# Four token tiles of an encoder trunk loaded column-major and normed there

## The chip, the cores and the metric

The kernel runs on one core of a Trainium2 chip. The metric is device time in microseconds (us) for one launch; lower is better. Each version is timed in several runs, and one further execution is recorded by the hardware profiler.

## The reference

One layer of a hybrid encoder over 1024 tokens (a grid of 16 x 64) with 1024 channels:

```python
h = layer_norm(x, emb_ln_g, emb_ln_b)
q, k, v, z_a, u, z_b, g_a, g_b = split(h @ w_in)          # 512 x6, 1024 x2 columns
y_a = neighbourhood_attention(q, k, v, rpb) * silu(z_a)   # 8 heads, windows of 8 x 16 keys
y_b = (rg_lru(conv(u), forward) + rg_lru(conv(u), backward)) * silu(z_b)
m = sigmoid(g_a + b0) * (y_a @ w_ba) + sigmoid(g_b + b1) * (y_b @ w_bb)
out = layer_norm(ALPHA * h + m @ w_out, ln_g, ln_b)
```

The embedding's norm h is needed twice: with channels on the partitions, as an operand of the input projection, and with tokens on the partitions, at the very end, in `ALPHA * h`.

## The kernel before

The tokens are cut into eight tiles of 128 (16 grid rows x 8 grid columns). A product of two float32 matrices is made from float32r halves: each operand is split into a high part (a cast, mostly on ScalarE) and a low part (the rest, a subtraction on VectorE or GpSimd), and three products are added up (`mm3`: high-high, low-high, high-low).

All engines work in the order in which the program text issues the instructions (TensorE, VectorE, ScalarE, GpSimd and the SP queue that issues DMAs are all scheduled by hand), so one line that waits holds up what stands behind it on its engine.

The first stage (0 to 82 us) norms the tokens and makes v and the first q heads. For a tile i of 4 to 7:

- `load_x(i)` loads 128 tokens x 1024 channels. `ln_sums` takes mean and variance on VectorE and a root on ScalarE; `ln_scale` applies them on ScalarE (L255); `ln_g` multiplies by the gain and adds the bias in four 128x512 operations on GpSimd (L261).
- `keep(i)` stores the result to `h_d` in DRAM, from where the last stage reads it.
- `turn` makes eight 128x128 transposes on TensorE into PSUM (L272, four for each half `kk` of the channels); `turn_hi` casts the high part on ScalarE (L281), `turn_lo` makes the low part on VectorE. They fill columns of `B11`, `B12`, `B21`, `B22`: first index, half of the channels; second, tiles 0 to 3 or 4 to 7.
- `t_full(i)` makes the sums of a Strassen-like scheme (seven block products instead of eight) on VectorE: t1, t2, t3 (L302 to L305), `t_last` t4; `t_hi` casts them on ScalarE (L314), `t_lo` makes the lows on GpSimd. They fill `T1` to `T4`.

Between these stand the products: `v_part(i, kind, ks)` ("h", "w", "a": high-high, low weights, low tokens; eight products each, L328), `q_part(m, n)`; their outputs are taken out of PSUM by `v_hi`/`v_lo`, `q_hi`/`q_lo` (ScalarE, VectorE L360). The outputs in the pool `ps0` take its four banks b0 to b3 as the list `places` deals them: v_part(2) to (7) take 3, 2, 3, 2, 0, 1 with q_part(1,0) on 1, and then q_part(0,1) 2 and q_part(1,1) 3. Before the block products, `s_load`, `s_sum` (VectorE, L386), `s_hi`, `s_lo` prepare the weights of pair 0.

The second stage (82 to 425 us) runs 17 pairs of weight columns, seven block products each (a11, a12, s2, s1, s3, s4, a22); a11 and a12 use B11 and B21, s2, s1, s3, a22 use T2, T1, T3, T4. Its PSUM pools `psd` (two banks) and `ps6` (six) take the place of `ps0` and `pst`.

The third stage (about 425 to 532 us) is attention, in units: 8 heads x 8 units, a unit being about 1.6 us. A unit has TensorE score one tile of the next head (`score`), turn a tile of probabilities (`turned`), multiply by values; VectorE adds the bias (`biased`) and makes lows, ScalarE takes exponentials (`exped`) and highs (`turned_hi`). `load_head` loads k, q and bias two heads ahead. Products of the other branch fill up TensorE. The last stage makes the output projection and the last norm; `z_load` reads `h_d`.

Lines that the profile gives as L128 are `lo_of`, a subtraction on whichever engine it is given; L134 is the product of `mm3`.

Of the kernel before, what the change touches and what calls it, by code (L numbers as in the profile page):

```python
# [10 lines left out]
F32 = mybir.dt.float32  # L11
# [24 lines left out]
HEAD_AT = 116  # L36
LO_POOL = ("a11", "a22")
# [9 lines left out]
SM_CW, SM_CB, SM_GB, SM_LAM, SM_BM, SM_N = 0, 16, 20, 36, 44, 60  # L47
# [20 lines left out]
def encoder_kernel(ctx, tc, x, gb1, gb, w_qk, w_v, w_s, w_ba, w_bb, w_gate, smalls, bias, w_out, out):  # L68
# [43 lines left out]
    smh = cst.tile([P, SM_N], F32, name="smh")  # L112
# [152 lines left out]

    tps = {}
# [27 lines left out]
    def t_full(i):  # L294
# [6 lines left out]
        A.copy(t3, tp4(i, 0))  # L301
        V.tensor_tensor(t1, tp4(i, 0), f(B11[0], i), ALU.subtract)  # L302
        V.tensor_tensor(t1, t1, f(B11[1], i), ALU.subtract)
        V.tensor_tensor(t2, tp4(i, 1), t1, ALU.subtract)
        V.tensor_tensor(t3, tp4(i, 1), t3, ALU.subtract)  # L305
# [63 lines left out]
    def s_load(p, *names):  # L369
        for z, o in enumerate(names if p < N_PAIR else ()):  # L370
            if p:
                t = wsp.tile([P, 4, P], F32, tag=o, bufs=2 if o == "a22" else 1, name=f"{o}_{p}f")[:]
            else:
                if z == 0:
                    place = dict(pool=ln, tag="x", bufs=5) if o == "a21" else dict(pool=wpl, tag="ws", bufs=1)
                    both = place.pop("pool").tile([P, 2, 4, P], F32, name=f"{o}_{p}f", **place)
                t = both[:, z]
# [86 lines left out]
    qk_load(1)  # L464
    load_x(6)
# [32 lines left out]
    for c, pl in zip((4, 3, 1, 2), hts):  # L498
        Ts[c] = pair(pl, [P, 4, HALF], f"ht{c}", tag=f"ht{c}")
    T1, T2, T3, T4 = (Ts[c] for c in (1, 2, 3, 4))  # L500
# [7 lines left out]
    def tile_in(i):  # L508
        for kk in BOTH:
            turned_in(i, kk)  # L510

# [4 lines left out]
    def ln_next(i):  # L516
        ln_sums(i)
        ln_scale(i)
        ln_g(i)

# [9 lines left out]
    ln_scale(4)  # L530
    ln_g(4)
    qk_prep(1)
# [5 lines left out]
    ln_next(5)  # L538
    for kind in "hwa":
        v_part(2, kind, KS)  # L540
    keep(4)
    ln_next(6)
    v_hi(2)
    for kind in "hw":
        v_part(3, kind, KS)
    v_lo(2)
    v_store(2)
    keep(5)
    tile_in(4)
    tile_lo(4)  # L550
    ln_next(7)
    v_part(3, "a", KS)
    t_full(4)
# [3 lines left out]
    keep(6)  # L557
    q_part(0, 0, slice(256, HALF))
    tile_in(5)
    q_hi(0, 0)  # L560
    t_hi(4, 2, 1, 3)
    t_lo(4, 2, 1, 3)
    tile_lo(5)
    q_lo(0, 0)
    q_store(0, 0)
    keep(7)
    t_full(5)
    q_part(1, 0)
    q_hi(1, 0)
# [3 lines left out]
    t_lo(5, 2, 1, 3)  # L573
    for kind in "hwa":
        v_part(4, kind, KS)
    tile_in(6)
    v_hi(4)
    tile_lo(6)
    v_lo(4)
    v_store(4)  # L580
    t_full(6)
    t_hi(6, 2, 1, 3)
    t_lo(6, 2, 1, 3)
    for kind in "hwa":
        v_part(5, kind, KS)
    s_load(0, "a11", "a12")
# [1177 lines left out]
```

## Time and profile before

| | |
|---|---|
| time, median of 3 runs | 663.57 us (663.17 to 663.83) |
| profiled execution, own time | 663.47 us |
| its span, first to last instruction | 661.7 us |
| granted TensorE clock | 0.997 |
| busy: PE / DVE / ACT / POOL | 649.3 / 524.5 / 388.7 / 395.6 us |
| DMA | 113.42 MB, 171 GB/s mean |

PE is TensorE's matmuls, PEld its weight loads, DVE VectorE, ACT ScalarE, POOL GpSimd, SP the queue that issues DMAs. A row of a timeline gives start, duration, engine, line, operation, output<-input and shape, and in brackets the idle time before it and what ended it. Equal instructions in a row are merged (x8); durations of neighbours overlap a little, so the distance of starts is what an instruction costs its engine.

### The profile page before, as it was taken

What the parts mean: (1) busy time and instruction counts of PE and PEld (TensorE: products, weight loads), DVE (VectorE), ACT (ScalarE), POOL (GpSimd) and SP (SyncE); (2) the same over time, 40 slices, a digit from 0 to 9 for tenths busy, and PEclk for the clock granted to TensorE, in tenths of its full rate; (3) what the DMA queues carried; (4) which work ended last, traced back from release to release, by engine and by line L of the source; (5) the groups of instructions that cost most, each with busy time, mean ns of one, the idle gap of its engine ahead of it and who ended that gap; (6) DMA issues with size and microseconds to landing.
All of it is one profiled execution on the core that took longest, in us unless ns stands there. A gap on an engine that the chain in (4) does not pass through costs nothing.

```text
span 661.7 us, 9467 instructions
## 1 busy us (share of the span) xinstructions
PE 649.3 (98%) x3119; PEld 542.3 (82%) x3119; DVE 524.5 (79%) x860; ACT 388.7 (59%) x686; POOL 395.6 (60%) x311
## 2 busy tenths in 40 slices
PE   8999999999999999999999999999999999999994
PEld 6888888888888888888788888889888888888883
DVE  7978767986899599879987697177887876994776
ACT  5564433356786677777666834277777734573242
POOL 6799263434676476658556455012552649989857
PEclk9999999999999999999999999999999999999998
DMA  8747607133334133532361548898977288333023
GB/s 326 275 140 247 192 33 230 42 113 125 128 115 140 48 112 108 180 109 83 132 218 60 191 161 286 302 350 272 355 267 243 66 307 295 111 115 127 24 104 128
DMA packets 52481, 113.42 MB, mean 171 GB/s; under 512 B 5504, under 2 KB 9936, under 8 KB 50896
## 3 DMA queue, kind: packets, MB, share of 16 engines
q1 hardware_dynamic: 51968, 112.28, 49.0%
q8 instruction: 25, 0.41, 0.3%
q10 hardware_dynamic: 464, 0.53, 0.2%
q14 instruction: 24, 0.20, 0.1%
HBM read 77.11 MB, written 35.68 MB: 170 GB/s over the span
## 4 chain that ended last, share of the span: by engine, by line
PE 87%; DVE 7%; POOL 2%; issue 1%; ACT 1%; DMA 0%; POOLq 0%; SPq 0%; DVEq 0%; ACTq 0%
PE a L134 32%; PE mb L134 13%; PE s L134 12%; PE x L134 6%; PE w L134 5%; PE v L328 4%; PE acc L1156 3%; PE s L1108 3%; PE pt L1130 3%; PE q L134 2%; PE g L806 2%; POOL x L261 1%; DVE ws_l L128 1%; PE tp L272 1%; DVE uc L764 1%
## 5 line engine op out<-in xcount | busy, mean ns | idle before, releaser
L134 PE MATMUL a<-ht_h,ws_h 128*128 128x512 f32 x136 | 53.1, 391 | 0.0
L134 PE MATMUL a<-ht_h,ws_l 128*128 128x512 f32 x136 | 53.0, 389 | 0.0
L134 PE MATMUL a<-b_h,wa_l 128*128 128x512 f32 x136 | 53.0, 389 | 0.0
L134 PE MATMUL a<-ht_l,ws_h 128*128 128x512 f32 x136 | 52.9, 389 | 0.0
L134 PE MATMUL a<-b_h,wa_h 128*128 128x512 f32 x136 | 52.9, 389 | 0.0
L134 PE MATMUL a<-b_l,wa_h 128*128 128x512 f32 x136 | 52.9, 389 | 0.0
L1118 DVE CUSTOM_DVE_ANT_0 sc<-s,bias 128x384 f32<-128x384 f32 (+1 forms) x64 | 33.4, 523 | 20.2 <-PE s L1108 9.1
L1137 ACT CAST pt_h<-pt 128x384 fp32r<-128x384 f32 x64 | 29.0, 453 | 23.8 <-PE pt L1130 19.3
L1123 ACT ACTIVATE p<-sc,summ 128x384 f32<-128x384 f32 (+1 forms) x64 | 37.9, 592 | 5.5 <-DVE summ L1118 5.1
L134 PE MATMUL mb<-ya,wb_h 128*128 128x512 f32 x128 | 39.7, 390 | 0.0
L914 POOL CAST wb_h<-wb 128x512 fp32r<-128x512 f32 x9 | 7.0, 779 | 48.2 <-DMA wb<-in_w_bb_dram 30.4
L128 DVE TENSOR_TENSOR pt_l<-pt,pt_h 128x384 fp32r<-128x384 f32 x64 | 33.2, 519 | 1.9 <-ACT pt_h L1137 1.5
L328 PE MATMUL v<-wv,b_h 128*128 128x512 f32 x128 | 32.6, 397 | 0.4 <-ACT b_h L427 0.4
L128 POOL TENSOR_TENSOR ht_l<-t,ht_h 128x512 fp32r<-128x512 f32 x16 | 22.0, 1407 | 18.3 <-ACT ht_h L314 18.3
L1522 POOL TENSOR_TENSOR z<-z,gb 128x512 f32<-128x512 f32 (+2 forms) x23 | 27.6, 1215 | 8.6 <-ACT z L1517 7.7
L1108 PE MATMUL s<-ks,qs 128*128 128x384 f32 (+1 forms) x128 | 31.6, 328 | 0.0
L134 PEld LDWEIGHTS a<-ht_h,ws_h 128*128 128x128 f32 x136 | 25.5, 188 | 5.9 <-issue 0.4
L1130 PEld LDWEIGHTS pt<-ident,p 128*128 128x128 f32 x176 | 23.2, 140 | 8.5
L134 PEld LDWEIGHTS a<-b_h,wa_h 128*128 128x128 f32 x136 | 25.5, 188 | 5.4
L134 PEld LDWEIGHTS a<-ht_l,ws_h 128*128 128x128 f32 x136 | 25.5, 188 | 5.4
L134 PEld LDWEIGHTS a<-b_h,wa_l 128*128 128x128 f32 x136 | 25.5, 188 | 5.3
L134 PEld LDWEIGHTS a<-b_l,wa_h 128*128 128x128 f32 x136 | 25.5, 188 | 5.3
(542 smaller groups left out, 2259.4 us busy)
## 6 DMA issues: line engine op xcount, KB each, us to landing
ks<-k_d SPq DMA_DIRECT2D x8, 1024.0 KB, 8.4
h_d<-x SPq DMA_DIRECT2D x8, 512.0 KB, 2.9
v_d<-vs SPq DMA_DIRECT2D x8, 512.0 KB, 3.2
q_d<-q SPq DMA_DIRECT2D x8, 512.0 KB, 3.2
ga_d<-ga SPq DMA_DIRECT2D x16, 256.0 KB, 2.1
gb_d<-gb SPq DMA_DIRECT2D x16, 256.0 KB, 2.5
k_d<-k SPq DMA_DIRECT2D x8, 512.0 KB, 4.0
qs<-q_d SPq DMA_DIRECT2D x8, 512.0 KB, 4.6
```

What stands on the lines that cost most here:

```text
L128: eng.tensor_tensor(lo, full, hi.bitcast(F32), ALU.subtract)
L134: PE.matmul(o, a, b, start=first and i == 0, stop=last and i == len(prods) - 1, skip_group_check=not (first and last))
L328: PE.matmul(vos[i][:], a, wv[kind == "w"][k][:], start=vn[i] == 0, stop=vn[i] == 23)
L806: PE.matmul(o[:, n, :], w[:, 2 * d + b, :], us[b][:, n * HALF:(n + 1) * HALF], start=z == 0, stop=z == 1)
L914: G.tensor_copy(hi[:], st[:])
L1108: PE.matmul(o[:, :P * len(near(t))], q[:, t * P:(t + 1) * P], k[:, z, keys], start=z == 0, stop=z == 1)
L1118: V.tensor_tensor_reduce(s[:, :w], o[:, :w], heads[h][2][:, b0:b0 + w], -1.0, 3.0e38, ALU.add, ALU.min, accum_out=sums[h][0][:, t:t + 1])
L1123: A.activation(probs[h % 2][t][:], scs.pop((h, t))[:, :w], AF.Exp, bias=sums[h][0][:, t:t + 1], scale=-1.0, accum_out=sums[h][1][:, t:t + 1])
L1130: PE.transpose(tp[:, n * P:(n + 1) * P], probs[h % 2][t][:, z * P:(z + 1) * P], ident[:])
L1137: A.copy(pt[0][:, span(b)], tps[h, b][:, :P * len(near(b))])
L1156: PE.matmul(acc[n][:, lo - n * HALF:hi - n * HALF], vvs[h // 2][:, b, h % 2, :], pt[:, a:a + hi - lo], start=b in (1, 6) and z == 0, stop= ...
L1522: G.tensor_tensor(z, z, gbs[c, n][:, part], (ALU.mult, ALU.add)[c])
```

## The change

Tiles 4 to 7 are also passed in transposed (`xt`, channels on the partitions) and loaded in that form; the token-major tile is still loaded, for its mean and variance alone. These two numbers per token are spread over all partitions by two TensorE transposes of a broadcast column (`spread`), copied to SBUF, and applied to the transposed tile by GpSimd (`centred`: subtract, multiply; four 128x512 operations). Gain and bias are per partition there and applied by ScalarE in eight 128x128 activations (`affine`), with the casts of the high part behind. The low parts (`lows_t`) and `t_full` then read the tile in SBUF. The eight transposes of these tiles, their `ln_scale`, `ln_g` and `keep` go.

The token-major normed form of tiles 4 to 7, which the last stage reads from `h_d`, is made in the attention stage, for 128 channels of all four tiles at a time (eight times, m): load, scale on ScalarE by the kept statistics, gain and bias on GpSimd, store. Several loads and `t_last` stand elsewhere in the order, and `finish_a` uses one buffer instead of two.

```diff
+TOKENS_AT = ((-2, 7, 8, 11), (4, 12, 13, 17))
...
+    def load_xt(i):
+        pl, tag = {4: (hts[3], "ht2h"), 5: (hts[0], "ht4h"), 7: (hts[0], "ht4l")}.get(i, (None, None))
+        if pl:
+            both_xt[0] = pl.tile([P, 2, NK, P], F32, tag=tag, name=f"xt{i}")
+        xts[i] = both_xt[0][:, int(i == 6)]
+        SP.dma_start(xts[i], xt[i - 4])
+    def stats_t(i):
+        ln_sums(i)
+        sts_rest(i)
+    def sts_rest(i):
+        ln_rstd(i)
+        st, mv, sd, ve = sts[i]
+        V.tensor_scalar(kept[:, 2 * i - 8:2 * i - 7], mv[:, 0:1], -1.0, sd, ALU.mult, ALU.mult)
+        V.tensor_copy(kept[:, 2 * i - 7:2 * i - 6], sd)
+    def spread(i):
+        bcp[i] = pst.tile([P, HALF], F32, tag="bank", name=f"bcp{i}")
+        for z, col in enumerate((sts[i][1][:, 0:1], sts[i][2])):
+            PE.transpose(bcp[i][:, z * P:(z + 1) * P], col.to_broadcast([P, P]), ident[:])
+    def centred(i):
+        bcs[i] = wsp.tile([P, 2, P], F32, tag=f"s{i - 3}", name=f"bc{i}")
+        A.copy(bcs[i][:], bcp[i][:, :2 * P].rearrange("p (z t) -> p z t", z=2))
+        for kk in range(2):
+            t = xts[i][:, 4 * kk:4 * kk + 4, :]
+            for z, op in enumerate((ALU.subtract, ALU.mult)):
+                G.tensor_tensor(t, t, bcs[i][:, z:z + 1, :].to_broadcast([P, 4, P]), op)
+    def affine(i):
+        for k in range(NK):
+            g, b = (sm[:, SM_LN + 8 * z + k:SM_LN + 8 * z + k + 1] for z in range(2))
+            A.activation(xts[i][:, k, :], xts[i][:, k, :], AF.Identity, bias=b, scale=g)
+            if k % 4 == 3:
+                A.copy(blocks[k // 4][1][0][:, :, ti(i)], xts[i][:, k - 3:k + 1, :])
+    def lows_t(i):
+        for kk in range(2):
+            hi, lo = blocks[kk][1]
+            lo_of(V, lo[:, :, ti(i)], xts[i][:, 4 * kk:4 * kk + 4, :], hi[:, :, ti(i)])
...
-        A.copy(t3, tp4(i, 0))
-        V.tensor_tensor(t1, tp4(i, 0), f(B11[0], i), ALU.subtract)
+        u0, u1 = xts[i][:, 0:4, :], xts[i][:, 4:8, :]
+        V.tensor_tensor(t1, u0, f(B11[0], i), ALU.subtract)
         V.tensor_tensor(t1, t1, f(B11[1], i), ALU.subtract)
-        V.tensor_tensor(t2, tp4(i, 1), t1, ALU.subtract)
-        V.tensor_tensor(t3, tp4(i, 1), t3, ALU.subtract)
+        V.tensor_tensor(t2, u1, t1, ALU.subtract)
+        V.tensor_tensor(t3, u1, u0, ALU.subtract)
...
+    def tokens_in(m):
+        cols = slice(m * P, (m + 1) * P)
...
+        SP.dma_start(hw[m][:], x[4:, :, cols].rearrange("i p c -> p i c"))
+        SP.dma_start(rows[0][:, m % 2], gb1[:, :, cols].broadcast_to([P, 2, P]))
+    def tokens_scaled(m):
+        for i in range(4):
+            A.activation(hw[m][:, i], hw[m][:, i], AF.Identity, bias=kept[:, 2 * i:2 * i + 1], scale=kept[:, 2 * i + 1:2 * i + 2])
+    def tokens_gained(m):
+        for z, op in enumerate((ALU.mult, ALU.add)):
+            G.tensor_tensor(hw[m][:], hw[m][:], rows[0][:, m % 2, z:z + 1].to_broadcast([P, 4, P]), op)
+    def tokens_out(m):
+        SP.dma_start(h_d[4:, :, m * P:(m + 1) * P].rearrange("i p c -> p i c"), hw[m][:])
...
+    for m in range(NK):
+        for unit, f in zip(TOKENS_AT[m % 2], (tokens_in, tokens_scaled, tokens_gained, tokens_out)):
+            todo.setdefault(16 * (m // 2) + unit, []).append(lambda f=f, m=m: f(m))
```

The new order of the first stage, from where the two differ (products at the places of before are left out where nothing around them changes; `qk_load(1)` is followed by `load_xt(4)`):

```python
load_xt(5); keep(2); keep(3)
...                                     # tiles 2 and 3 turned; ln_sums(4); v_lo(0)
sts_rest(4); tile_lo(2); tile_lo(3); v_lo(1); v_store(1)
load_x(7); load_xt(6); load_xt(7)
v_part(2, "h"); v_part(2, "w"); spread(4); centred(4); qk_prep(1); stats_t(5)
v_part(2, "a"); stats_t(6); v_hi(2); v_part(3, "h"); spread(5); centred(5); v_lo(2); v_store(2)
v_part(3, "w"); spread(6); centred(6); stats_t(7); affine(4)
v_part(3, "a"); lows_t(4); t_full(4); v_hi(3); v_lo(3); v_store(3)
q_part(0, 0, second half); spread(7); centred(7); affine(5); q_hi(0, 0)
t_hi(4, 2, 1, 3); t_lo(4, 2, 1, 3); q_lo(0, 0); q_store(0, 0); lows_t(5); t_full(5)
q_part(1, 0); affine(6); q_hi(1, 0); q_lo(1, 0); q_store(1, 0)
t_hi(5, 2, 1, 3); t_lo(5, 2, 1, 3); lows_t(6); t_full(6); t_last(4); s_load(0, "a11", "a12")
v_part(4); affine(7); v_hi(4); t_hi(6, 2, 1, 3); t_lo(6, 2, 1, 3); s_load(0, "a21", "a22"); v_lo(4); v_store(4)
v_part(5); lows_t(7); t_full(7); v_hi(5); v_lo(5); t_last(5); s_load(1, "a21"); v_store(5)
t_hi(7, 2, 1, 3); t_lo(7, 2, 1, 3)
v_part(6); s_sum(0, ...); v_hi(6); v_lo(6); s_load(1, "a12"); v_store(6)
v_part(7); v_hi(7); v_lo(7); s_load(1, "a11"); v_store(7)
...                                     # s_hi, s_lo of pair 0, q_part(0, 1), q_part(1, 1) as before
t_hi(4, 4); t_hi(5, 4); t_last(6); t_last(7); t_hi(6, 4); q_hi(1, 1); q_lo(1, 1); q_store(1, 1); t_hi(7, 4)
t_lo(4..7, 4)
```

More of the change, by code (lines that the diff above doesn't have):

```diff
@@ L464, in encoder_kernel @@
     qk_load(1)
+    load_xt(4)
     load_x(6)
@@ L537, in encoder_kernel @@
     load_x(7)
[L538 to L542, printed above, removed]
+    load_xt(6)
+    load_xt(7)
+    v_part(2, "h", KS)
+    v_part(2, "w", KS)
+    spread(4)
+    centred(4)
+    qk_prep(1)
+    stats_t(5)
+    v_part(2, "a", KS)
+    stats_t(6)
     v_hi(2)
-    for kind in "hw":
-        v_part(3, kind, KS)
+    v_part(3, "h", KS)
+    spread(5)
+    centred(5)
     v_lo(2)
     v_store(2)
[L548 to L551, printed above, removed]
+    v_part(3, "w", KS)
+    spread(6)
+    centred(6)
+    stats_t(7)
+    affine(4)
     v_part(3, "a", KS)
+    lows_t(4)
     t_full(4)
```

105 lines of the change are left out of this document (55 added, 50 removed).

## The prediction

> **What bounds the kernel now.** I read the page's busy times first, then TensorE's waits, then the timeline of each engine over 16 to 100 us, the only stretch whose order changes apart from attention.
>
> ```profile
> PE 649.3 (98%) x3119; PEld 542.3 (82%) x3119; DVE 524.5 (79%) x860; ACT 388.7 (59%) x686; POOL 395.6 (60%) x311
> ...
> PE a L134 <- DVE w L839: 0.4, 1, 0.4
> ...
> PE tp L272 <- POOL x L261: 0.3, 1, 0.3
> ...
> 4.01 2.74 PE L213 MATMUL gps<-ident,gb_col 128*128 128x128 f32 x16
> 6.58 0.50 PE L204 MATMUL clock<-zero 128*128 128x128 bf16 x6
> ...
> 26.39 3.92 PE L328 MATMUL v<-wv,b_h 128*128 128x512 f32 x16
> 30.14 1.98 PE L328 MATMUL v<-wv,b_l 128*128 128x512 f32 x8
> ...
> 41.18 0.60 PE L272 MATMUL tp<-ident,x 128*128 128x128 f32 x4
> 42.10 0.66 PE L272 MATMUL tp<-ident,x 128*128 128x128 f32 x4 [0.32 <-POOL x L261]
> 42.51 0.48 PE L134 MATMUL q<-b_h,wqk_h 128*128 128x512 f32 x1
> ...
> 48.07 3.79 PE L328 MATMUL v<-wv,b_h 128*128 128x512 f32 x16
> ...
> 53.51 1.03 PE L272 MATMUL tp<-ident,x 128*128 128x128 f32 x8
> 54.30 3.92 PE L328 MATMUL v<-wv,b_h 128*128 128x512 f32 x16
> ...
> 82.53 0.39 PE L134 MATMUL a<-b_h,wa_h 128*128 128x512 f32 x1
> ...
> 85.25 0.39 PE L134 MATMUL a<-b_h,wa_h 128*128 128x512 f32 x1
> ```
>
> TensorE is busy for 98% and after its first 10 us it waits twice, 0.32 us at tile 5's transposes and 0.4 for a scan's input near 320. So the time falls by what TensorE no longer issues, as long as the other engines still feed it in time; every wait that appears counts in full. In the timeline, columns are start, duration, engine, line, op; starts of neighbours give the true price: eight transposes of a tile take 54.30 - 53.51 = 0.79 us.
>
> **What TensorE saves.** 32 transposes go: three tiles at 0.79, and tile 5 at 42.51 - 41.18 = 1.33 with its wait, 3.70 us. Two transposes of a broadcast column per tile come, eight in all. Their nearest row is the 16 of L213, (6.58 - 4.01)/16 = 0.16 us each; if the slow ones were only a cold start, they cost the 0.10 us of an ordinary transpose. So 0.8 to 1.3 us return, and TensorE alone gains 2.4 to 2.9; I take 2.6. Without any wait the first product a11 would start at 79.9 instead of 82.53 and a12 at 82.65 instead of 85.25.
>
> **What the others get instead.** ScalarE loses a 128x1024 scaling and a copy per tile, and gains the copy of the two broadcast rows and eight 128x128 activations. GpSimd keeps four 128x512 operations a tile (centre and scale instead of gain and bias). VectorE keeps its count but not its operands: the lows of both halves and three of t_full's four subtractions read the transposed tile from PSUM until now, and from SBUF afterwards. That is the edit which matters, for these rows:
>
> ```profile
> 50.21 2.98 POOL L261 TENSOR_TENSOR x<-x,gb 128x512 f32<-128x512 f32 x2
> ...
> 51.58 1.62 POOL L261 TENSOR_TENSOR x<-x,gb 128x512 f32<-128x512 f32 x1
> ...
> 50.09 0.68 DVE L302 TENSOR_TENSOR t<-tp,b_h 128x512 f32<-128x512 f32 x1
> 50.80 1.24 DVE L303 TENSOR_TENSOR t<-t,b_l 128x512 f32<-128x512 f32 x1
> 52.08 0.69 DVE L304 TENSOR_TENSOR t<-tp,t 128x512 f32<-128x512 f32 x1
> ...
> 81.82 0.69 DVE L310 TENSOR_TENSOR t<-t,b_l 128x512 f32<-128x512 f32 x1
> ...
> 186.05 1.75 POOL L128 TENSOR_TENSOR wa_l<-a_5f,wa_h 128x512 fp32r<-128x512 f32 x1
> 188.78 1.74 POOL L128 TENSOR_TENSOR wa_l<-a_6f,wa_h 128x512 fp32r<-128x512 f32 x1
> 186.56 1.78 DVE L386 TENSOR_TENSOR s_6f<-a_6f 128x512 f32<-128x512 f32 x1
> ```
>
> L302, L303 and L304 have one shape and run beside GpSimd. The two that read PSUM take 0.68 and 0.69 us; the one with both operands in SBUF takes 1.24, and GpSimd's operation beside it takes 1.62 instead of 1.3. The same form takes 0.69 (L310) while GpSimd rests. So the two engines take turns: VectorE waits for the running GpSimd operation, then the next one of GpSimd waits for VectorE. Where both have a queue (186 us), each takes about 1.75. VectorE's 0.60 us operation then costs 1.75.
>
> Before, four of VectorE's two-SBUF operations (L303), and the first two sums of s_sum, met GpSimd; the rest ran while it was idle:
>
> ```profile
> 34.41 2.39 POOL L128 TENSOR_TENSOR wqk_l<-wqk_s,wqk_h 128x1024 fp32r<-128x1024 f32 x1
> 36.76 16.44 POOL L261 TENSOR_TENSOR x<-x,gb 128x512 f32<-128x512 f32 x12
> 53.16 11.76 POOL L128 TENSOR_TENSOR ht_l<-t,ht_h 128x512 fp32r<-128x512 f32 x9
> 66.92 4.25 POOL L128 TENSOR_TENSOR ht_l<-t,ht_h 128x512 fp32r<-128x512 f32 x3 [2.01 <-ACT ht_h L314]
> 87.43 5.95 POOL L128 TENSOR_TENSOR ht_l<-t,ht_h 128x512 fp32r<-128x512 f32 x4 [16.26 <-ACT ht_h L314]
> ...
> 69.01 1.01 DVE L386 TENSOR_TENSOR s_0f<-a_0f 128x512 f32<-128x512 f32 x1
> 70.05 1.67 DVE L386 TENSOR_TENSOR s_0f<-s_0f,a_0f 128x512 f32<-128x512 f32 x1
> ...
> 77.96 0.69 DVE L360 SCALAR_TENSOR_TENSOR q<-q,q 128x512 fp32r<-128x512 f32 x1 [1.44 <-ACT q L355]
> ...
> 83.36 0.69 DVE L360 SCALAR_TENSOR_TENSOR q<-q,q 128x512 fp32r<-128x512 f32 x1 [0.84 <-ACT q L355]
> ...
> 59.51 1.66 ACT L314 CAST ht_h<-t 128x512 fp32r<-128x512 f32 x3 [3.10 <-DVE t L304]
> ...
> L1137 ACT CAST pt_h<-pt x64: 359/479/482, 435.5 to 530.4; 128x384 fp32r<-128x384 f32 x48, 128x256 fp32r<-128x256 f32 x16
> ```
>
> **The walk.** I go through the new order of each in-order engine by hand: GpSimd 1.29 us per 128x512, VectorE 0.60, 1.75 each when both queue, ScalarE 0.24 per 128x128 (0.36 and 0.48 at 256 and 384 columns leave 0.12 per 128) and 0.53 per 128x512 cast. Up to tile 7's statistics little changes. spread(4) stands behind the 16 products of v_part(2) from 26.39, at 30.1; with 0.4 for it and 0.4 for the copy, centred(4) starts on GpSimd at 31.0 and ends at 36.15, and qk_lo (2.39) ends at 38.5. Tile 7's statistics are no longer behind tile 4's lows; their root is off ScalarE at 39.0, and affine(4) follows there until 41.9.
>
> From here VectorE's queue sets the pace, since GpSimd always has centred(5), (6), (7) and then the twelve t_lo operations waiting. VectorE ends lows_t(4) at 43.4, t_full(4) at 50.4, v_lo(3) and q_lo(0,0) at 51.6, lows_t(5) at 53.9, t_full(5) at 60.9, q_lo(1,0) at 61.5, lows_t(6) at 64.4, t_full(6) at 70.3 (GpSimd is briefly empty there), t_last(4) at 72.6, v_lo(4) at 73.2, lows_t(7) at 76.1: 22 two-SBUF operations in 35 us, where they would take 13 alone.
>
> TensorE against it: v_part(4) at 47.1 and v_part(5) at 52.5 find their lows. v_part(6) reaches its low products near 61.6 and waits for lows_t(6), about 1.9 us in two pieces. v_part(7) reaches its low products at 69.0 and waits for lows_t(7), 5.4 us and then 0.8; it ends at 77.1, before near 71.6 (82.53 less two q_parts of 5.44, the price of 24 products by 53.51 - 48.07). q_part(0,1) takes the PSUM bank of v_part(5) (the list `places` deals 2, to both), which v_lo(5) behind t_full(7) frees at 79.1. It and q_part(1,1) take 10.9 us and end at 90.05.
>
> VectorE goes on: t_last(5) against t_lo(7) to 82.1, s_sum to 85.7, v_lo(6), v_lo(7) to 86.9, five s_lo to 89.9, q_lo(0,1) 90.8, two s_lo 91.95, then t_last(6) and t_last(7) beside T4's lows on GpSimd to 97.8, and q_lo(1,1) to 98.4. After `ps0` and `pst` are given up, `psd` takes banks 0 and 1, so a11 falls on bank 2 (q_part(0,1)) and a12 on bank 3 (q_part(1,1)). Before, these were free at 78.65 and 84.05, ahead of 82.53 and 85.25. Now a11 waits until 90.85 and a12 until 98.45. T1 to T3 end by 83.3 and T4 near 99, ahead of their products (a22 comes 16 us behind a11). Sum: 98.45 - 85.25 = 13.2 us later, the 2.6 gain already inside.
>
> **The queues.** SP: load_xt(4) goes after qk_load(1) at 20 us, xt 5, 6, 7 in place of four stores of h_d, 512 KB for 512 KB; xt(4) has eleven us until GpSimd reads it at 31, more than the 9.1 that twice as many bytes (ks, below) needed at most. What stands behind x(7) on SP are xt(6), xt(7), ahead of v_store(2) only, which no one waits for until q_hi. Nothing charged. kept adds one 128x1 operation per tile on VectorE, about 0.2, inside the walk.
>
> **Attention.** Eight times a load of 256 KB and rows of 128 KB, four 128x128 activations, two GpSimd operations, a store.
>
> ```profile
> 446.00:459.00 13.00, 13.00 (x82) 11.58 (x82) 10.36 (x30) 9.60 (x28) 1.90 (x2) 1.00 0.80 270
> 459.00:472.00 13.00, 13.00 (x82) 11.41 (x81) 10.60 (x32) 9.57 (x27) 10.67 (x10) 1.00 0.97 347
> ...
> 436.02 1.46 SPq L936 DMA_DIRECT2D ks<-k_d  x1
> ...
> DMA to landing us min/median/max: 5.0/8.4/9.1
> ...
> 447.21 0.40 PE L1108 MATMUL s<-ks,qs 128*128 128x256 f32 x2
> ```
>
> The columns are PE, PEld, DVE, ACT, POOL, clock, DMA share, GB/s. ScalarE has 3.4 us free of 13 and gets 1.2 at one time, behind exped, with the next turned_hi 0.5 to 1.1 us off; GpSimd has 8 us free in every 25; VectorE's operations there read PSUM, so GpSimd does not slow them. The DMA share is the tight one: ks of head 2 lands by 445.1 at the slowest, 2.1 us ahead of its use at 447.21, and 384 KB put in front of it take 384/340 = 1.1 us. The SP queue can wait for a store that is still in flight before it reloads the same tile (three slots, 4.7 us, later), with a reload that is first read over seven slots on. Charged at 0, bound 1.5, and below by 0 as nothing on TensorE's path is taken away here.
>
> **Sum.** 663.47 (the profiled execution; span 661.7 and 1.8 around it; 0.1 under the median of the runs) + 13.2 = 676.7 us.
>
> **Rivals.**
> Only one of the two bank waits binds: the buffers fall otherwise than I read them, or VectorE's chain is a few us shorter because GpSimd loses turns. Then a11 sets the shift, 90.85 - 82.53 = 8.3: 671.8 us, with a spread from 665 to 673. For it: no wait on a bank shows in this trace; against: the banks' order follows from the list.
>
> It is faster, 660.9 us (660.4 to 661.8): VectorE's chain stays ahead of TensorE, so only the 2.6 counts. The point from which this decides is lows_t(7) at 67 and q_lo(1,1) at 82.6, so 43 two-SBUF operations and nine that read PSUM (31 us alone) must fit into 42 us from 40.5; that is so if an operation costs under 0.85 instead of 1.75. For it: all sums of VectorE's and GpSimd's own work fit, L303's first took 1.02 only. Against: every row where both queue.
>
> The saved transposes are hidden or eaten to the last (no change): the chain's end would have to hit 85.2 by chance.
>
> Slower still: TensorE runs slowly after a long stop. The 16 transposes at 4 us took 0.16 each, those at 53 us 0.10; at that rate for the 5 us from its first work at 1 us to 6 us, a restart loses 5 x (1 - 0.10/0.16) = 1.9. Only the stop in front of a12 (4.9 us) is on the path: 678.6 us. The Trainium skill's "TensorE: Matmul & The Clock Gate", Part 1, says that the array halves its clock after an idle window of about 3.4 us and needs as long to return; by that, an estimate of 1.7 us would be lost. No stop of such length after the start is in this trace, so it stays a rival.
>
> **Chances.** The walk, with and without the slow restart, 673 to 681: 0.45 (0.12 of it the restart). One bank wait or a shorter chain, 665 to 673: 0.28. Faster: 0.20. Within 0.2%, which is about what a measurement can tell from no change: 0.05. Above 681: 0.02. Slower by over 0.2%: 0.75. 673 to 681 and 665 to 673 alone hold 0.73, so the range has to reach to the faster case: 660.5 to 680.0. The forecast's own range is 673 to 680.
>
> **What would show it.** Right: VectorE's t and b_l subtractions between 41 and 76 us at 1.2 to 1.8 us each, GpSimd's at 1.6 to 1.75; TensorE waiting for VectorE at v near 62 and 70, and at a near 91 to 98; VectorE's q_lo(1,1) after 90. Tile transposes gone and eight column transposes at 0.10 to 0.16. Wrong: those subtractions at 0.7 beside a busy GpSimd, or no TensorE wait over 1 us before 100 us; a wait of s for ks or of pt for VectorE past 430 us would be a cost that I put at nothing.

## The result and the profile after

The changed kernel takes 687.39 us (median of 5 runs, 686.06 to 689.05) against 663.38 of the kernel before: a ratio of 1.0363, interval 1.0342 to 1.0385. It is slower, as forecast, but by 24.0 us instead of 13.2, and outside the range. Its profiled execution took 688.78 us, with a span of 686.7.

The busy times and the DMA packets from the page of the changed kernel come first:

```profile
PE 658.1 (96%) x3095; PEld 541.3 (79%) x3095; DVE 542.0 (79%) x864; ACT 407.2 (59%) x746; POOL 421.5 (61%) x327
...
DMA packets 63104, 118.66 MB, mean 173 GB/s; under 512 B 5888, under 2 KB 20560, under 8 KB 61520
```

The busy times alone say little: TensorE has 24 matmuls fewer and is yet busy for 8.8 us more, VectorE for 17.5. To see where 25.0 us of span went, both executions are cut at the same four events: the first product that reads a T tile (s2), the first score, the first product of ya (the start of the product stage), and the last of them. Columns: stretch and its length, busy us and instructions of PE, PEld, DVE, ACT and POOL, granted clock, DMA share, GB/s. First the kernel before, then the changed one:

```profile
0.00:88.00 88.00, 85.42 (x448) 71.75 (x448) 71.42 (x141) 48.07 (x88) 58.18 (x49) 1.00 0.65 228
88.00:428.60 340.60, 340.22 (x1494) 279.41 (x1493) 276.03 (x322) 205.77 (x264) 189.77 (x140) 1.00 0.40 139
428.60:532.30 103.70, 103.52 (x642) 91.60 (x642) 80.52 (x229) 76.21 (x215) 40.01 (x39) 1.00 0.75 259
532.30:575.80 43.50, 43.50 (x194) 35.80 (x193) 34.35 (x51) 21.65 (x40) 37.04 (x31) 1.00 0.70 243
575.80:661.70 85.90, 76.65 (x350) 63.78 (x348) 62.19 (x119) 37.02 (x81) 70.57 (x55) 0.98 0.30 102
```

```profile
0.00:99.90 99.90, 87.49 (x423) 69.59 (x423) 89.36 (x144) 55.65 (x116) 68.36 (x52) 0.98 0.55 195
99.90:441.40 341.50, 340.52 (x1493) 279.54 (x1493) 274.96 (x323) 206.00 (x264) 184.99 (x137) 1.00 0.41 140
441.40:553.00 111.60, 106.40 (x640) 92.44 (x641) 80.65 (x229) 86.65 (x247) 60.52 (x55) 0.98 0.85 284
553.00:599.10 46.10, 45.25 (x193) 35.92 (x192) 34.80 (x52) 22.11 (x41) 36.81 (x31) 1.00 0.69 235
599.10:686.70 87.60, 78.39 (x350) 63.84 (x348) 62.28 (x118) 36.79 (x81) 70.80 (x55) 0.96 0.29 99
```

The loss is 11.9 us in the first stage, 0.9 in the second, 7.9 in attention, 2.6 in the product stage and 1.7 in the output stage. Only the first stage was in the forecast.

The clock of 0.98 in the first stage and in attention (1.00 before) stands for one spell in each: the granted clock falls from 1.00 to 0.50 for 3.4 us, from 75.3 us on behind a wait of 2.83 us, and from 502.0 us on behind one of 2.11. In a spell TensorE does 1.7 us less work. Eight products at full clock, eight like them in the first spell, and the 13 us (columns as above) that hold the second:

```profile
57.65 2.02 PE L376 MATMUL v<-wv,b_l 128*128 128x512 f32 x8
...
74.87 3.76 PE L376 MATMUL v<-wv,b_l 128*128 128x512 f32 x8 [2.83 <-DVE b_l L130]
...
497.00:510.00 13.00, 10.89 (x60) 9.54 (x59) 7.23 (x22) 7.08 (x21) 5.86 (x5) 0.87 0.82 269
```

What TensorE waits for in the changed kernel (total, times, longest):

```profile
PE v L376 <- DVE b_l L130: 5.4, 3, 2.8
PE s L1161 <- DMA ks<-k_d: 3.9, 3, 2.1
PE a L136 <- ACT u L1042: 2.3, 1, 2.3
PE q L136 <- DVE vs L130: 1.2, 1, 1.2
...
PE mb L136 <- POOL wb_l L130: 0.9, 1, 0.9
PE a L136 <- DVE q L408: 0.7, 1, 0.7
```

The first stage is in the timeline (start, duration, engine, line). L130 is the subtraction of lows_t and t_lo, L300 centred, L350 to L353 t_full, L357 and L358 t_last:

```profile
38.88 18.34 POOL L300 TENSOR_TENSOR xt<-xt,bc 128x512 f32<-128x512 f32 x12
63.59 4.66 POOL L130 TENSOR_TENSOR ht_l<-t,ht_h 128x512 fp32r<-128x512 f32 x3 [1.28 <-ACT ht_h L362]
70.98 4.97 POOL L130 TENSOR_TENSOR ht_l<-t,ht_h 128x512 fp32r<-128x512 f32 x3 [2.73 <-ACT ht_h L362]
...
46.23 1.78 DVE L350 TENSOR_TENSOR t<-xt,b_h 128x512 f32<-128x512 f32 x1
48.05 1.68 DVE L351 TENSOR_TENSOR t<-t,b_l 128x512 f32<-128x512 f32 x1
49.76 1.66 DVE L352 TENSOR_TENSOR t<-xt,t 128x512 f32<-128x512 f32 x1
...
68.83 0.69 DVE L351 TENSOR_TENSOR t<-t,b_l 128x512 f32<-128x512 f32 x1
69.56 0.69 DVE L352 TENSOR_TENSOR t<-xt,t 128x512 f32<-128x512 f32 x1
...
97.07 1.65 DVE L358 TENSOR_TENSOR t<-t,b_l 128x512 f32<-128x512 f32 x1
...
98.76 0.62 ACT L362 CAST ht_h<-t 128x512 fp32r<-128x512 f32 x1 [2.28 <-DVE t L358]
99.28 0.58 ACT L1042 COPY u<-a 128x512 f32<-128x512 f32 x1
```

At 48.05 and 49.76 GpSimd is inside its 18 us of centring; the same two lines at 68.83 and 69.56 fall between its groups, and take 0.69. The last three rows show what s2 stood for: the copy of a11's bank on ScalarE, behind the last cast of T4, behind t_last(7).

### The profile page after: what moved, and what is told of

Same layout as the page of the kernel before. It is cut to its first block, busy times and chain, and to the rows that moved or that the text cites. A ratio compares the mean times of both kernels' runs of the same rounds, so it can differ in the third digit from the quotient of the medians.

```text
span 686.7 us, 9525 instructions
## 1 busy us (share of the span) xinstructions
PE 658.1 (96%) x3095; PEld 541.3 (79%) x3095; DVE 542.0 (79%) x864; ACT 407.2 (59%) x746; POOL 421.5 (61%) x327
## 4 chain that ended last, share of the span: by engine, by line
PE 70%; DVE 11%; DMA 10%; issue 4%; POOL 2%; ACT 2%; SPq 1%; POOLq 0%; DVEq 0%; ACTq 0%
PE a L136 30%; PE s L136 12%; PE mb L136 8%; PE x L136 6%; PE w L136 5%; DMA ks<-k_d 3%; PE s L1161 2%; PE g L859 2%; PE v L376 2%; DVE b_l L130 2%; PE acc L1209 1%; PE pt L1183 1%; DMA rs_d<-rs 1%; DMA g<-gb_d 1%; DMA wvsl<-in_w_v_dram 1%
## 5 line engine op out<-in xcount | busy, mean ns | idle before, releaser
L1171 DVE CUSTOM_DVE_ANT_0 sc<-s,bias 128x384 f32<-128x384 f32 (+1 forms) x64 | 33.4, 523 | 24.6 <-PE s L1161 13.2
L130 POOL TENSOR_TENSOR ht_l<-t,ht_h 128x512 fp32r<-128x512 f32 x16 | 26.0, 1651 | 17.9 <-ACT ht_h L362 17.9
L130 DVE TENSOR_TENSOR pt_l<-pt,pt_h 128x384 fp32r<-128x384 f32 x64 | 33.1, 519 | 4.8 <-ACT pt_h L1190 4.8
L1288 POOL TENSOR_TENSOR hw<-hw,ln_rows 128x512 f32<-128x512 f32 x16 | 20.6, 1289 | 24.6 <-DMA g<-gb_d 15.4
L1183 PEld LDWEIGHTS pt<-ident,p 128*128 128x128 f32 x176 | 22.8, 140 | 10.2 <-DVE pt_l L130 1.6
L1183 PE MATMUL pt<-ident,p 128*128 128x128 f32 x176 | 30.0, 274 | 0.7 <-DVE pt_l L130 0.7
```

The lines of the kernel that those rows point to most:

```text
L130: eng.tensor_tensor(lo, full, hi.bitcast(F32), ALU.subtract)
L1171: V.tensor_tensor_reduce(s[:, :w], o[:, :w], heads[h][2][:, b0:b0 + w], -1.0, 3.0e38, ALU.add, ALU.min, accum_out=sums[h][0][:, t:t + 1])
L1183: PE.transpose(tp[:, n * P:(n + 1) * P], probs[h % 2][t][:, z * P:(z + 1) * P], ident[:])
L1288: G.tensor_tensor(hw[m][:], hw[m][:], rows[0][:, m % 2, z:z + 1].to_broadcast([P, 4, P]), op)
```

## The experiments

The stages of all kernels, in us, cut as above, with the medians (before: 663.3 to 663.7 in every group):

| kernel | median | ratio, interval | first | second | attention | product | output |
|---|---|---|---|---|---|---|---|
| before | 663.4 | | 88.0 | 340.6 | 103.7 | 43.5 | 85.9 |
| changed | 687.4 | 1.0342 to 1.0385 | 99.9 | 341.5 | 111.6 | 46.1 | 87.6 |
| e1_first_stage | 678.6 | 1.0211 to 1.0242 | 99.8 | 341.3 | 103.9 | 44.8 | 87.3 |
| e2_attention | 675.5 | 1.0166 to 1.0209 | 89.0 | 340.9 | 110.8 | 45.5 | 87.4 |
| l2_before_shift | 667.8 | 1.0045 to 1.0075 | 88.8 | 340.9 | 103.7 | 45.1 | 87.6 |
| l1_after_pad | 683.6 | 1.0283 to 1.0313 | 99.6 | 340.4 | 110.2 | 45.3 | 85.9 |
| e3_psum | 681.6 | 1.0254 to 1.0289 | 92.4 | 341.1 | 112.6 | 46.3 | 87.6 |
| e9_no_centring | 682.2 | 1.0266 to 1.0302 | 94.4 | 341.3 | 110.7 | 45.8 | 87.6 |
| e8_one_norm | 678.0 | 1.0203 to 1.0238 | 88.7 | 343.1 | 112.7 | 46.1 | 87.6 |
| e7_split | 689.1 | 1.0358 to 1.0406 | 100.1 | 342.9 | 109.4 | 47.2 | 87.5 |
| e4_rows | 684.6 | 1.0303 to 1.0338 | 99.3 | 341.4 | 106.0 | 47.9 | 87.3 |
| e5_dma_only | 686.7 | 1.0314 to 1.0363 | 99.0 | 341.1 | 113.2 | 44.8 | 87.5 |
| e6_second | 691.2 | 1.0395 to 1.0430 | 99.3 | 354.3 | 103.9 | 44.8 | 87.4 |
| e10_late_rsb | 689.1 | 1.0367 to 1.0420 | 99.0 | 341.2 | 111.9 | 46.1 | 87.6 |
| e11_free_sp | 701.7 | 1.0547 to 1.0591 | 99.6 | 341.4 | 121.0 | 51.0 | 87.4 |
| c2_second | 674.3 | 1.0137 to 1.0177 | 92.9 | 345.8 | 103.7 | 43.4 | 85.7 |
| c3_rows | 676.9 | 1.0181 to 1.0215 | 93.6 | 340.9 | 108.6 | 44.9 | 85.6 |

The stages are those of one profiled execution each. One spell of the halved clock lies in attention in the changed kernel, e2, e5, e8, e9 and c3 and in the second stage in e7 and e8; e6's second stage and e11's attention and product stage have longer ones. Six kernels with the same attention program (changed, l1, e3, e7, e8, e9) took 109.4 to 112.7 us for it, so the 7.9 us there are 5.7 to 9.0, and differences of less than some 3 us say little.

**The two halves apart.** e1_first_stage: `for m in range(0)` around the token work of attention, and `keep(i)` of the raw tiles in the first stage.

> The changed kernel with its first stage as it is and nothing of the moved token-major work: the attention stage loads, norms and stores no tokens, and the raw tiles 4 to 7 are stored from the first stage as the kernel before stored the normed ones. It leaves out the token-major norm of tiles 4 to 7. Theory (two separate losses): the first stage keeps its loss, s2 near 100 us (88.0 before, 99.9 in the changed kernel), and the attention stage is back from 111.6 to 104 us, so the time is 675 to 678 us. Rival A (the attention loss comes from something else that the change touched there, such as the single buffer of the value copies, or from TensorE being slower after the idle time of the first stage): 684 to 688 us. Rival B (the first stage's loss is given back later once attention is undisturbed): 664 to 670 us.

e2_attention: the kernel before with the token work of attention and without keep(4) to keep(7), and with what goes with it: the changed sizes of the constants and the one buffer of `finish_a`.

> The kernel before with the moved work alone: tiles 4 to 7 are turned and normed in the first stage as before, but their token-major normed form is not stored there; it is loaded raw, normed and stored in the attention stage, exactly as in the changed kernel. Theory (two separate losses): first stage as before (s2 near 88 us), attention 110 to 112 us instead of 103.8, with the waits for ks behind it; time 671 to 676 us. Rival A (the attention loss is only a result of the late or slowed first stage): 663 to 665 us. Rival C (the first stage also gains from having no stores of its own, so part is given back): 667 to 670 us.

Each half costs by itself: 15.3 us the first, 12.2 the second. Attention is at 103.9 without the token work and at 110.8 with it, whatever the first stage did. But the two add up to 27.5, more than 24.0, and the product and output stages are longer in both, which have no work in common there. In e1, 0.6 us above its expected band, these two stages hold 2.7 us of the loss.

**The place in memory.** Those stages have matmuls of 392 to 399 ns instead of 389. What e1 and e2 share is in the head of the program: the change cuts `smh` from 60 columns to 16, adds `kept` (8) and lengthens `sm` by 16, so all that is allocated behind them moves.

```
-    smh = cst.tile([P, SM_N], F32, name="smh")
+    smh = cst.tile([P, 16], F32, name="smh")
+    pad = cst.tile([P, 24], F32, name="pad")
```

> The kernel before with one thing else: the constants at the start of the on-chip memory take 80 bytes less per partition, as in the changed kernel, so that everything behind them lies 80 bytes lower (a start that is a multiple of 16 and no longer of 32 bytes). Nothing that is computed differs. It asks where the 2.5 to 3 us come from that the product stage after attention and the output stage are longer in all five changed kernels so far, with matmuls at 392 to 399 ns instead of 389. Theory (the place of the operands): product stage 44.8 us instead of 43.5, output stage 87.3 instead of 85.9, time 665.5 to 667 us. Rival (the slower pace follows from the waits before, by the clock): 663.0 to 664.0 us.

l1_after_pad is the changed kernel with a `pad` of 20 columns.

> The changed kernel with 80 unused bytes per partition among the constants, so that the operands of the left side of the on-chip memory start again where they start in the kernel before (the first operand at byte 1760 instead of 1664; the right side ends at the same place in all kernels, so left and right have again the same remainder of 128). Nothing else. Theory (the placement of left against right operands slows the matmuls whose two operands lie on the two sides): mb stage loses 1.6 us, the output stage 1.7 us, the stages before 0.8 to 1.1 us; matmuls of the output stage at 389 ns again; time 682.5 to 684.5 us. Rival (in the changed kernel the pace follows from the waits before): 686.5 to 688 us.

The rows of the product and output stages, in the kernel before, in l2_before_shift and in l1_after_pad (count, then shortest, median and longest ns):

```profile
L134 PE MATMUL mb<-ya,wb_h x128: 387/389/497, 532.3 to 575.8; 128*128 128x512 f32 x128
...
L134 PE MATMUL x<-t2h,s2h x16: 389/389/389, 597.7 to 607.9; 128*128 128x512 f32 x16
```

```profile
L136 PE MATMUL mb<-ya,wb_h x128: 392/397/496, 533.4 to 578.5; 128*128 128x512 f32 x128
...
L136 PE MATMUL x<-t2h,s2h x16: 389/392/396, 601.0 to 611.3; 128*128 128x512 f32 x16
```

```profile
L138 PE MATMUL mb<-ya,wb_h x128: 388/389/505, 550.2 to 595.5; 128*128 128x512 f32 x128
```

That the place costs time is shown, and more than expected: the kernel before, computing the same in the same order (with one memset of the padding more), becomes 4.4 us slower by the shift (0.8 in the first stage, 0.3 in the second, 1.6 in the product stage, 1.7 in the output stage). The changed kernel is 3.8 us faster without it. In the traces the product stage is 0.8 and the output stage 1.7 us shorter in l1; the 1.4 in attention go with the spell of halved clock that l1 does not have there. Two statements in the expectations do not hold in detail. The compiled program starts every tile at a multiple of 32 bytes, so the 80 bytes became 96 (first operand from 1760 to 1664, as the second expectation has it) and the starts stayed multiples of 32; no trace shows an address. And operands on two sides are not the whole of it: t2h and s2h both lie in pools of the left side in both kernels and slowed down all the same. Why a place is slow stays open.

**The first stage.** e3_psum writes the normed column-major tile into PSUM, so that lows_t and t_full read one operand there:

```
-            A.activation(xts[i][:, k, :], xts[i][:, k, :], AF.Identity, bias=b, scale=g)
+            A.activation(tp4(i, k // 4)[:, k % 4], xts[i][:, k, :], AF.Identity, bias=b, scale=g)
```

> The changed kernel with one thing else: ScalarE writes the normed column-major tile to a PSUM bank (and t3 is copied from it, one 128x512 copy more per tile on ScalarE), so that the subtractions of lows_t and t_full read one operand from PSUM, as in the kernel before. Theory (VectorE takes turns with GpSimd where both of its operands lie in SBUF): these subtractions go from 1.66-1.78 us back to about 0.6 us, and GpSimd's centring from 1.65 to about 1.4 us; s2 at 86 to 90 us, time 674 to 678 us, since the attention part stays. Rival D (ScalarE's longer column-wise norm and the order of its queue set the first stage): no gain, or 1 to 3 us more than the changed kernel: 686 to 691 us.

e9_no_centring cuts GpSimd's operations to `t[:, :, 0:16]`.

> The changed kernel with GpSimd's sixteen centring and scaling operations of the first stage on 16 of each block's 128 columns instead of all (it leaves out the centring of the others); VectorE's subtractions still read both operands from the on-chip memory. Theory (these take long only while GpSimd works at the same time): lows_t and t_full at about 0.7 us where GpSimd stands, and, with GpSimd's 19 us gone, s2 at 90 to 93 us instead of 99.9; time 677 to 681 us. Rival (two operands in the on-chip memory are slow for VectorE by themselves): these stay at 1.5 to 1.8 us, s2 at 97 to 100 us, time 684 to 688 us.

From e9's timeline, the same lines as above, for tile 4 and for tile 5:

```profile
45.07 0.68 DVE L350 TENSOR_TENSOR t<-xt,b_h 128x512 f32<-128x512 f32 x1
45.79 0.69 DVE L351 TENSOR_TENSOR t<-t,b_l 128x512 f32<-128x512 f32 x1
46.52 0.69 DVE L352 TENSOR_TENSOR t<-xt,t 128x512 f32<-128x512 f32 x1
...
54.07 1.78 DVE L350 TENSOR_TENSOR t<-xt,b_h 128x512 f32<-128x512 f32 x1
...
45.19 2.94 POOL L300 TENSOR_TENSOR xt<-xt,bc 128x64 f32<-128x64 f32 x4 [4.38 <-ACT bc L296]
50.60 4.70 POOL L130 TENSOR_TENSOR ht_l<-t,ht_h 128x512 fp32r<-128x512 f32 x3 [2.47 <-ACT ht_h L362]
```

The three operations that took 1.66 to 1.78 us in the changed kernel take 0.69 with the same operands in the same place; tile 5's still takes 1.78, beside GpSimd's low parts. So GpSimd's work at the same time makes them long, not their place. That is what the Trainium skill's "SBUF — State Buffer", section "SBUF: two separate sides", states of a VectorE instruction with two SBUF inputs against a GpSimd one that reads SBUF; the 0.69 against 1.66 to 1.78 us agree. e9's time (682.2 us) and its first stage (94.4) missed the expected 677 to 681 and 90 to 93: GpSimd's lows of T1 to T3 now run where the centring did, beside VectorE's next tiles.

In e3_psum the first stage is 7.5 us shorter, not the 10 to 14 expected, and its time 681.6 lies between the theory's band and the rival's. Its next limit shows in ScalarE's groups, 8 norms and 2 casts and a copy for each tile:

```profile
L307 ACT ACTIVATE tn<-xt,sm 128x128 f32<-128x128 f32 x32 | 14.9, 465 | 0.8
...
L330 ACT CAST b_h<-tn 128x512 fp32r<-128x512 f32 x8 | 4.7, 587 | 0.3
...
L351 ACT COPY t<-tn 128x512 f32<-128x512 f32 x4 | 2.4, 597 | 0.0
```

Two tries at that queue. e7_split gives four of eight norms to VectorE (`V.tensor_scalar` for `k % 4 < 2`); e8_one_norm makes one 128x512 norm of four.

> The kernel with the normed column-major tile in PSUM (e3_psum, 681.6 us), with four of the eight column-wise norms of each tile on VectorE instead of ScalarE. Theory (with the shared-operand cost gone, ScalarE's queue of eight norms, two casts and a copy per tile, 6 us, is what the rest of the first stage's loss waits for): ScalarE 2 us shorter per tile, VectorE 1 us longer; s2 at 89 to 91 us instead of 92.4, time 678 to 680 us. Rival (VectorE is as full as ScalarE, or the rest of the loss is only the copy of a11's bank that stands behind the last casts of T4): 681 to 685 us.

> The kernel with the normed column-major tile in PSUM (e3_psum, 681.6 us, s2 at 92.4 us) with the eight column-wise norms of a tile on ScalarE replaced by two operations of 128x512 with one column's gain and bias for all (it leaves out the gains and biases of the other columns). Theory (ScalarE's queue of eight norms, two casts and a copy sets what is left of the first stage's loss): 8 x 0.47 = 3.8 us per tile becomes 2 x 0.6 = 1.2 us; s2 at 88 to 90 us, time 677 to 680 us. Rival (the rest of the loss is the copy of a11's bank behind the last casts of T4): s2 at 92 us, time 681 to 682 us.

e8's first stage falls by 3.7 to 88.7 us, as the theory said. e7 was 7.5 us slower than e3_psum, beyond its own rival: these rows are from its groups and its waits,

```profile
L308 DVE TENSOR_SCALAR tn<-xt,sm 128x128 f32<-128x128 f32 x16 | 6.2, 410 | 0.3
```

```profile
PE v L381 <- ACT b_h L333: 6.7, 3, 3.5
```

VectorE took 0.41 us for each norm, little less than ScalarE, and the cast of a bank now stood behind two in-order queues.

**Attention.** e5_dma_only keeps the transfers and leaves out the engines' part; e4_rows cuts the same work into runs of 1 KB (two tiles by 256 channels); e6_second moves it into the second stage as whole rows.

> The changed kernel with the token transfers of the attention stage as they are and neither ScalarE's scaling nor GpSimd's gain there (it leaves out the token-major norm of tiles 4 to 7; the raw tiles are loaded and stored back). Theory (the transfers alone make the attention stage longer): attention stays at 110 to 112 us, time 685 to 688 us. Rival F (the 32 scalings on ScalarE and 16 gain operations on GpSimd, 31 us together, delay what the scores need): attention back to 104 to 106 us, time 679 to 682 us.

> The changed kernel with the late token work cut another way: two tiles by 256 columns instead of four tiles by 128 columns, so runs of 1 KB instead of 512 B in the token loads, the token stores and the gain rows (which are loaded four times instead of eight, the same bytes in all), with the same bytes, the same engine work and the same places in the order. Theory (the DMA engines are full in attention, and what fills them is the number of 512 B packets): half of the 10,240 added packets are gone, some 5,100; attention falls from 111.6 to 105-109 us, and the time is 680 to 685 us. Rival E (it is the bytes): within 1 us of the changed kernel, 686 to 689 us. Rival F (ScalarE's and GpSimd's added work): the same, 686 to 689 us, with the waits for ks unchanged.

> The changed kernel with the late token work moved from the attention stage to the first fifteen or so of the products of the second stage, where the DMA engines are 41% busy, and cut in whole rows (4 KB runs) in buffers that the recurrence uses only later. Same function. Theory (the token transfers cost only where the DMA engines are full): attention back to 104 us; the second stage, where GpSimd has 185 of 341 us of work, takes the 21 us of gain operations with 0 to 3 us of waits; time 677 to 682 us. Rival (GpSimd's turns with VectorE or its lateness with the low parts of the operands make waits there): second stage 5 us or more longer, time 683 to 690 us.

Transfers alone do it: attention is 113.2 us in e5, a little above what was expected. Half the packets with the same bytes give back 5.6 of 7.9 us in e4, of which 1.7 is the spell that e4 does not have. The two kernels with runs of 1 KB, e4 at 106.0 and c3 below at 108.6, lie under all those with 512 B, so the size of the packets is a large part of it; how large, one trace of each does not settle. Of e4's gain 1.8 is lost again in the product stage, where it waits for wb_h (1.4) and wb_l (0.9, as in the changed kernel). In e6 attention is at 103.9, but the second stage is 12.8 us longer, as its rival had it, though not by its mechanism alone: ScalarE stood for loads that I had placed only two products ahead.

```profile
ACT hw L1015 <- DMA hw<-in_x_dram: 14.9, 3, 6.3
```

What waits for what inside attention is in the SP queue's waits, first of the kernel before, then of the changed one, then the landing of the keys in the changed one (issue to landing, us):

```profile
SPq L1187 <- DMA rs_d<-rs: 18.2, 8, 5.3
```

```profile
SPq L1240 <- DMA rs_d<-rs: 24.8, 4, 7.8
SPq L1279 <- DMA h_d<-hw: 14.7, 3, 5.6
```

```profile
DMA to landing us min/median/max: 9.5/9.6/10.8
```

The SP queue stands longer for the small store of the sums and, as a new wait, for the token store before it can load tokens into the same buffer; and the keys behind it land later (before: 5.0 to 9.1). In all it stands no longer than before (69 against 72 us in the stage): before, 30.6 of that was for ScalarE's sums, for which it came early, and now 6.6. Two runs should tell the stand from the landing. e10_late_rsb moves `sums_in` of even heads behind the next `load_head`:

> The changed kernel with one transfer moved on the SP queue: for the even heads the spread reload of the reciprocal sums (rsb), which stands until their 4 KB store has landed, is issued behind the loads of the head after next (queries, bias, keys) instead of ahead of them. The bytes and packets stay. Theory (with the DMA engines full, the store lands late, SP stands for it, and the keys behind it come too late): half of the heads' keys are issued some microseconds earlier, the waits for ks (3.9 us) fall to 0 to 2 us, attention from 111.6 to 107-110 us, time 683 to 686 us. Rival (the keys are late because their own 1 MB transfer takes longer): ks waits stay, time 686 to 689 us.

e11_free_sp does so for all heads but the last, with the gates three units and the token loads two units later:

> The changed kernel with the SP queue freed ahead of the keys: the spread reload of every head's reciprocal sums but the last stands behind the next head's loads, two to five score units later than before (the gates' product with them on GpSimd three units later), and the token loads stand two units later, so that no reload waits for a store just issued. e10_late_rsb moved the even heads only, and its keys were issued no earlier than the changed kernel's (35.7 and 49.6 us after the first score, there 36.1 and 49.1): the queue stood at the odd heads' reload and at the token load instead. Theory (the standing queue, not the keys' own transfer, makes the keys late): keys issued 32 to 34, 45 to 47 and 58 to 60 us after the first score, waits for ks 0 to 1 us, attention from 111.6 to 105-108 us, time 681 to 684 us. Rival (the transfers themselves: the engines are full, and keys take 9.5 to 10.8 us to land instead of 5.0 to 9.1): ks waits of 3 us or more stay, attention 110 to 112 us, time 685.5 to 689 us.

Neither did. In e10 the keys were issued when they had been, since the queue still stood at the odd heads' reload, and attention stayed at 111.9; its rival expected that too, so nothing follows. In e11 the waits for ks are gone, but GpSimd's gates came late and the attention outputs with them, and the queue still stood 18.3 us for token stores:

```profile
PE acc L1209 <- DVE attn L1220: 6.8, 2, 6.6
...
PE mb L136 <- POOL wb_h L967: 4.8, 1, 4.8
```

The trace of the changed kernel says more for the first keys that came too late, since TensorE had not waited inside the stage until then:

```profile
477.11 0.67 SPq L989 DMA_DIRECT2D ks<-k_d  x1
...
486.65 0.51 PE L1161 MATMUL s<-ks,qs 128*128 128x256 f32 x2 [0.86 <-DMA ks<-k_d]
```

They were issued 35.7 us after the first score, before the change 31.0, and landed after 9.5 us, before after 8.4 (the median): 5.8 us of lateness made a wait of 0.9, so there was room for about 5, and neither part alone would have made TensorE wait. How the rest of the 7.9 us divides between the late issue and the slower landing stays open; that the added transfers alone cause both is shown by e5.

**A better version.** c2_second and c3_rows join the repairs: norm into PSUM, 80 bytes of padding, t_last(6) and (7) earlier, and token work in the second stage (loads four products ahead) or in 1 KB runs.

> Candidate: the normed column-major tile in PSUM; the 80 unused bytes; t_last of tiles 6 and 7 ahead of the first sums' low parts on VectorE, so that the casts of T4 and the copy of a11's bank behind them come earlier; and the late token work as whole rows in the second stage, with ScalarE's scaling four products behind each load instead of two (in e6_second ScalarE stood 14.9 us for these loads). Expected, if the three causes are apart: s2 at 89 to 92 us, second stage 341 to 345, attention 104, product stage 43.5 to 44.5, output stage 85.9: time 665 to 671 us. Rival (GpSimd's 24 us of gain operations make waits in the second stage whatever the distance): second stage 348 us or more, time 672 to 680 us.

> Candidate: the normed column-major tile in PSUM; the 80 unused bytes; t_last of tiles 6 and 7 earlier on VectorE, as in c2_second; and the late token work in the attention stage in runs of 1 KB (e4_rows). Expected: s2 at 89 to 92 us, second stage 341, attention 106, product stage 44 to 46.3, output stage 85.9: time 667 to 673 us. Rival (with the first stage earlier the attention stage's transfers wait as in e3_psum, 112.6 us): 674 to 678 us.

Both beat the changed kernel and neither the kernel before; both missed their band and lie in their rival's, though neither rival's mechanism fits (second stage 345.8 instead of 348 or more, attention 108.6 instead of 112.6). In c2 the product stage, the output stage and attention are back where they were; the second stage keeps 5.2 us. In both the earlier t_last only exchanged the wait for u (2.3 us) against one for q_lo (3.0), behind which a spell of halved clock cost a11 and a12 another 1.7, and in c3 attention, with a spell of its own, gave back 4.0 instead of 6.6 us against e3_psum.

## Why the prediction was wrong

**One step failed and one was missing.** The step that failed is the charge of 0, bound 1.5, for attention: it cost 7.9 us. The prediction sized the new load by its bytes at the stretch's mean rate (384 KB, 1.1 us) against a slack of 2.1 us, as one late transfer, and trusted that the SP queue's reload could wait because it is read late. Both halves of that were mis-sized. In the trace, TensorE stands for 5.0 us more in the stage (3.9 for the keys), the spell of halved clock costs 1.7, and 1.2 are not traced. These rows are the main queue over the attention stage (packets, MB, share of 16 engines' time) of the kernel before, the changed one and e4_rows:

```profile
q1 hardware_dynamic: 7807, 26.61, 74.6%
```

```profile
q1 hardware_dynamic: 17900, 31.58, 85.0%
```

```profile
q1 hardware_dynamic: 12933, 31.52, 86.0%
```

The added transfers kept all engines busy for 0.850 x 111.6 - 0.746 x 103.7 = 17.5 us. By an estimate from these rows, if the other transfers took what they took before, that is 17.5 x 16 / 10,093 = 28 ns of one engine for each packet of 512 B, against (0.860 x 106.0 - 0.746 x 103.7) x 16 / 5,126 = 43 ns for one of 1 KB. And the queue is in order: what matters in the reload's wait is not who reads the tile, but that keys stand behind it.

The missing step: three sizes of constants at the head of the program were not priced at all, not even at nothing. They cost 4.4 us by l2_before_shift.

The sum by the runs: 11.1 in the first stage (11.9 less 0.8 of place), 7.9 in attention and 4.4 of place, 23.4 of 25.0; of the rest 0.9 is the product stage's wait for wb_l and 0.6 the second stage's wait for m ahead of the first score.

**The walk of the first stage was right**, in direction and mechanism, and nearly in size, the last in part by luck: 13.2 forecast, 11.9 at s2, 0.8 of this from elsewhere. Operations of 1.75 us are there at 1.66 to 1.78; the waits for lows_t began at 63.4 and 72.0 (forecast 61.6 and 69.0) and took 2.6 and 2.8 us instead of 1.9 and 6.2; q_lo(0,1) ended at 91.8 (90.8) and q_lo(1,1) at 99.3 (98.4). The rival "faster" needed 0.85 us for an operation, and fell with that. TensorE's own gain was about the 2.6 charged: in e8, where its other waits are short (0.6 us more than in the kernel before), a11 starts at 80.7, which without the place's 0.8 is the 79.9 worked out.

Smaller steps were wrong in it. The column-wise norm takes 0.47 to 0.48 us instead of 0.24 (0.42 from start to start); e8 shows what that would cost next, 3.7 us, once VectorE is faster. The second bank wait did not come: a12 started 2.8 us behind a11, at 94.7, and s2 waited instead, for the copy of a11's bank. So a12 was 9.5 us late, not 13.2, and the size came near because another wait, which the walk does not have, hangs on t_last(7) too: that is the luck in it. The rival of one bank wait was right on the bank and wrong on the time. The slow restart of the other rival did occur, at shorter waits and at another place than it names. The spell at 75.3 us costs nothing, as TensorE stands another 1.18 us for VectorE right behind it, and kernels with 10.2 us of halved clock in this stage (e4, e5, e10) reach s2 at 99.0 to 99.3; the one in attention costs 1.7, near the 1.9 that the rival worked out for one restart.

## What to carry to other kernels

Count an added transfer by its packets as well as its bytes, in the stage where it runs, and then ask what stands behind its waits on the in-order queue that issues it. Before an operand is moved from PSUM to SBUF to save TensorE work, look at what GpSimd does at that moment: 0.69 us became 1.7. And when a change resizes a constant, move only the constant once, as a control: here that alone was 0.6%, nearly a fifth of the whole loss, most of it in stages that the change never touched.

## What the runs showed of the hardware

Matmuls of one shape took 389 ns or 392 to 399 ns (medians) according to where the program's tiles lie, by a shift of 96 bytes; nothing in the waits or in the granted clock (1.00 in both over the product stage) gives it away, only the rows' median.

By the estimates above, transfers in 512 B runs moved 18 bytes per ns on an engine (512/28), those in 1 KB runs 24 (1,024/43). The Trainium skill's "DMA: Bandwidth & Descriptors", section "Specifications", names 512 B as the least size for the full rate; here runs of twice that size moved some 30% more by the estimate, and the measurement decides.

In every run with TensorE waits of over 2.3 us, the granted clock fell to 0.50 at least once, for 3.4 us or a multiple of it, and TensorE did up to 1.7 us less work in each 3.4. The length of the wait before it did not decide: c3 had a spell behind a wait of 1.85 us, the changed kernel none behind 2.30 us at s2, and l1 none behind 3.15 us in attention.

VectorE's per-column scale and bias of 128x128 into PSUM took 0.41 us, ScalarE's 0.47, against 0.68 for a subtraction of 128x512 on VectorE and 0.59 for a cast of 128x512 on ScalarE: a quarter of the elements takes over half of the time on both.
